# Rounded weight halves brought by a converting DMA on the Pool queue, with every fourth remainder subtracted on GpSimd

## The chip, the core and the metric

The kernel runs on one core of one Trainium2 chip. The metric is the time on the device, in microseconds, from the start of the program to its end. The matrix engine (TensorE, "PE" in the profile), the vector engine (VectorE, "DVE"), the scalar engine (ScalarE, "ACT"), GpSimd ("POOL") and the engine that issues most DMAs (SyncE, "SP") run side by side and wait for one another through semaphores. Sixteen DMA engines move the data between device memory and the on-chip memory.

## The reference

The program is a two-layer transformer trunk over 256 tokens of width 2048, all in float32. What matters here is that nearly all of the work is products of a small activation with large weights, each of which is used once.

```python
# x: (1, 256, 2048); layer 0: gated linear attention + MLP, layer 1: stick-breaking attention + MLP
h = x
h = h + gla_mixer(rms_norm(h, norm1_g[0]), gla_w_in[0], ..., gla_w_out[0])
h = h + jnp.square(jax.nn.relu(rms_norm(h, norm2_g[0]) @ mlp_w_up[0])) @ mlp_w_down[0]
k_sh, v_sh = shared_kv(h, kv_norm_g, kv_w)
h = h + stick_breaking_mixer(rms_norm(h, norm1_g[1]), sb_w_q[0], k_sh, v_sh, sb_w_out[0])
h = h + jnp.square(jax.nn.relu(rms_norm(h, norm2_g[1]) @ mlp_w_up[1])) @ mlp_w_down[1]
return rms_norm(h, final_g)        # mlp_w_up: (2, 2048, 8192), mlp_w_down: (2, 8192, 2048)
```

## The kernel before

Every weight is cut into units of 1 MB, 128 partitions by 2048 float32 values. The list `plan` holds the 361 units in the order of their use: 49 of the linear attention's input, 16 of its output, 128 of the first MLP, 8 and 16 of keys, values and queries, 16 of the second output projection, and 128 of the second MLP. SP loads a unit into a tile `raw`, of which there are three.

TensorE multiplies float32 data in a form with a short mantissa (float32r). To keep the precision, each weight is used as the sum of two such numbers. Each unit is taken as two halves of 128x1024. For a half, `prefetch` makes `wh`, the weight rounded to float32r (line 147, a cast on ScalarE), and `wl`, the remainder `raw - wh` (line 148, a subtraction on VectorE). There are three buffers of `wh` and three of `wl`. `next_half` calls `prefetch` until three halves are ready, and takes the first. So the buffers of half i+3 are those of half i, and they come free when TensorE has ended half i.

The activations are split in the same way, and stand as `[high | low]` beside each other. A unit whose weights are stationary (`unit_t`: names `up`, `qk`, `sq`, `sk`, lines 169 and 172) runs two matmuls for each of its 16 blocks of 128 rows: `wh` against 512 columns, `wl` against 256. A unit whose weights move (`half_n`: names `dn`, `op`, `v`, `r`, `sv`, lines 202 to 204) runs three matmuls of 512 columns for each pair of a block and a token tile: low tokens by `wh`, high tokens by `wh`, high tokens by `wl`. So in either kind both parts are needed almost as soon as a half begins: `wl` is read by the first, the second or the third matmul.

The MLP runs in four passes for each layer: 16 units `up` (each followed by `joined`, the sum of two halves of a PSUM bank: a copy `lo` on ScalarE, line 187, and the sum `s` on VectorE, line 188, then the squared ReLU `y` and its split into `hT`), and 16 units `dn` (each chunk of four followed by two additions to `h`, line 572). Other work (attention scores, norms) is handed out in steps by `pump` between the weight products. The last eight halves have buffers of their own (`stay`), because the last chunk runs one token tile after the other.

The order on each engine is that of a scheduler, which starts from the order of the code. Each engine works its own list in that order, and an instruction that waits holds up all that stand behind it on its engine.

Of the kernel before, what the change touches and what calls it, by code (L numbers as in the profile page):

```python
# [8 lines left out]
F32 = mybir.dt.float32  # L9
# [4 lines left out]
ALU = mybir.AluOpType  # L14
# [25 lines left out]
def yoco_kernel(ctx: ExitStack, tc: tile.TileContext, a: dict):  # L40
    nc = tc.nc
    V, S, PE = nc.vector, nc.scalar, nc.tensor

    # one table set serves every function used here
    S.preload_act_table_set("natural_log_exp_and_others")
# [6 lines left out]
    half = ctx.enter_context(tc.tile_pool(name="half", bufs=4))  # L52
# [5 lines left out]
    def t512(name, dt=F32):  # L58
        return tmp.tile([P, 512], dt, tag="t512", name=name)

    def t256(name):
        return half.tile([P, T], F32, tag="t256", name=name)
# [4 lines left out]
    def act_tile(name, pool=None):  # L67
        return (pool or actp).tile([P, KT, 2 * T], F32R, tag="act", name=name)

# [1 line left out]
    pending = []  # L71
    given = [0]
# [9 lines left out]

    # the first n given out so far have to be complete
    def drain(n=None):
        while pending and (n is None or given[0] - len(pending) < n):
            pump()
# [4 lines left out]

    # ---- weights: every unit is loaded whole, then split in halves, exactly, into a
    # 12-bit part and the rest; splits are issued ahead of the products that use them ----
    def out_order(w):
        return [w[c, i] for c in (0, 1) for i in range(3)] + [w[c, 3] for c in (0, 1)] + \
            [w[c, i] for c in (2, 3) for i in range(4)]
# [8 lines left out]
    plan = []  # L105
# [14 lines left out]
    before, between = {}, {}  # L120

    def prefetch():
        i = state["n"]
        if i == 2 * len(plan):
            return
        state["n"] += 1
        if i % 2 == 0:
            for todo in before.pop(i // 2, []):
                todo()
            raw = wraw.tile([P, 2048], F32, tag="raw", name="raw")  # L130
            for lo, hi in ((0, 512), (512, 1024), (1024, 2048)) if i == 0 else ((0, 2048),):
                nc.sync.dma_start(raw[:, lo:hi], plan[i // 2][:, lo:hi])
                for todo in between.pop((i, hi), []):
                    todo()
            state["raw"] = raw
        part = state["raw"][:, (i % 2) * 1024:(i % 2 + 1) * 1024]
        last = i - 2 * len(plan) + 8
        if last < 0:
            wh = wsp.tile([P, 1024], F32R, tag="wh", name="wh")
            wl = wsp.tile([P, 1024], F32R, tag="wl", name="wl")  # L140
        else:
            # the last chunk's products come one token tile after the other: all its weights stay
            if last == 0:
                state["stay"] = [act_tile(n).rearrange("p k t -> p (k t)") for n in ("stay_h", "stay_l")]
            wh, wl = [b[:, last * 1024:(last + 1) * 1024] for b in state["stay"]]
        for lo, hi in ((0, 512), (512, 1024)) if i == 0 else ((0, 1024),):
            S.copy(wh[:, lo:hi], part[:, lo:hi])  # L147
            V.tensor_tensor(wl[:, lo:hi], part[:, lo:hi], wh[:, lo:hi].bitcast(F32), op=ALU.subtract)  # L148
        ready.append((wh, wl))
# [8 lines left out]

    # out[feature, token]: weights stationary, [high | low] tokens moving
    def unit_t(act, name, steps=1):  # L160
# [22 lines left out]

    # sum of the two halves of a bank
    def joined(ps, out, rows=P):
        lo = t256("lo")
        S.copy(lo[0:rows], ps[0:rows, T:2 * T])  # L187
        V.tensor_tensor(out, ps[0:rows, 0:T], lo[0:rows], op=ALU.add)  # L188

    # out[token, column chunk]: tokens stationary, weights moving  # L190
    def banks(name):
        return [psA.tile([P, 512], F32, tag="psA", name=f"{name}{t}") for t in range(NT)]
# [23 lines left out]

    # a tile as the sum of two that the tensor engine takes in one pass
    def split(src, tile):
        hi, lo = tile("hi"), tile("lo")
        S.copy(hi, src)  # L220
        V.tensor_tensor(lo, src, hi.bitcast(F32), op=ALU.subtract)
        return hi, lo
# [8 lines left out]

    # 1 / sqrt(u), one Newton step behind the tables
    def rsqrt(u, out):
# [9 lines left out]

# [1 line left out]
    ident = const.tile([P, P], F32, name="ident")  # L245
    ones = const.tile([P, P], F32, name="ones")
# [19 lines left out]

# [1 line left out]
    xg = act_tile("xg")  # L268
# [48 lines left out]

    # a value per token, from partitions to the free axis of all partitions
    def spread(col, out, scale):
# [6 lines left out]

    # transposed, scaled and split: what the next products read
    def feed(c, targets):
# [29 lines left out]

# [1 line left out]
    oT = act_tile("oT")  # L360

    # scores of one head: decayed queries and keys, level by level; every exponent is at most 0
    def scores(hd, qT, kT, st, sx):
# [21 lines left out]

        # between the two token tiles, and on the diagonal
        e = t512("e0").rearrange("p (f t) -> p f t", f=2)
# [19 lines left out]

        # within them: keys of a pair's first half against queries of its second
        for lv, s in enumerate(LEVELS):
            if lv % 4 == 0:  # L410
                ps = psm("lev").rearrange("p (l t c) -> p l t c", l=4, t=NT)
            n = min(4, len(LEVELS) - lv // 4 * 4)
# [27 lines left out]

    # outputs of one head, its norm, the gate
    def outputs(hd, st, sx, vv, gs):
# [42 lines left out]

    # the output gate times the head's gain
    def gates(pss):
# [117 lines left out]

# [1 line left out]
    rstd, _ = squared_rstd(ssq, "rstd2")  # L607
# [26 lines left out]

    # one group of heads; keys on partitions, (head, query) along the free axis
    def sticks(n, qs):
        heads = slice(n * GRP, (n + 1) * GRP)

        # scores of a key tile against a query tile
        def score(qt, kt):  # L640
# [11 lines left out]

        # softplus, split: the products below have a side of ones and zeros
        def soft(z):
# [7 lines left out]

        # less everything between the key (itself too) and the query
        def weigh(z, own, later=None):
# [45 lines left out]
    for n in range(KVH):  # L710
        qs = [t512(f"q{t}") for t in range(NT)]
        for g in range(GRP):
            ps = unit_t(xq, "sq", 1 + (len(pending) > 1 or g == GRP - 1))
            s = t256("s")
# [50 lines left out]

# ---- layouts: stationary units [feature tile][partition][k tile, 128], moving units
# [1 line left out]
def _stationary(w):  # L768
# [17 lines left out]
def _lay_out(i):  # L786
# [27 lines left out]
    r["final_g"] = np.ascontiguousarray(i["final_g"])  # L814
    # constants of the shapes alone
    r["ident"] = np.eye(P, dtype=np.float32)
    at = np.arange(P)
# [4 lines left out]
    for s in LEVELS:  # L822
        second = at[at // s % 2 == 1][None, :]
# [20 lines left out]
```

## Time and profile before

| | |
|---|---|
| time, median of 2 runs | 2115.03 us (2114.76 to 2115.30) |
| span of the profiled execution | 2113.3 us |
| PE busy | 2097.4 us, 99% of the span |
| weight loads of PE (PEld) | 1763.1 us, 83% |
| DVE busy | 1313.0 us, 62% |
| ACT busy | 1039.5 us, 49% |
| POOL busy | 0.2 us |
| DMA moved | 388.40 MB, mean 184 GB/s |
| casts `wh`, line 147 | 715 + 8, 1051 ns each |
| subtractions `wl`, line 148 | 715 + 8, 1224 ns each |

Some instruction records overlap in time on PE, so its busy time is an upper reading. An engine's busy time says how much it does, and not whether anything waits for it; that is read from the waits and from the chain that ended last. The span leaves out about 1.7 us around the program that the time of a run contains.

### The profile page before, as it was taken

Reading aid. Unit: us, or ns where it says so; the run is one execution under the profiler, and the core shown is the slowest. Engines: PE = TensorE matmul, PEld = TensorE weight load, DVE = VectorE, ACT = ScalarE, POOL = GpSimd, SP = SyncE. Lnnn points to the kernel's source line nnn. Section 1 sums busy time; section 2 is a strip of 40 time slices with the busy share of each in tenths; the row PEclk is TensorE's granted clock in tenths of the full one; section 3 lists DMA queues with packets and bytes.
Section 4 is the critical chain, followed back from the end, with each engine's and each line's share of the span. In section 5 each row is a group of like instructions: output and inputs, shape, how many; then the busy total and the mean of one; then the engine's idle time right before and its main releaser. Section 6 shows DMA issues by size and latency. Waiting matters only on the chain.

```text
span 2113.3 us, 26650 instructions
## 1 busy us (share of the span) xinstructions
PE 2097.4 (99%) x10544; PEld 1763.1 (83%) x10544; DVE 1313.0 (62%) x1804; ACT 1039.5 (49%) x1447; POOL 0.2 (0%) x4
## 2 busy tenths in 40 slices
PE   8999999999999999999999999999999999999998
PEld 7888888888888888888888888888888888888886
DVE  5767876665566556556666687666556546655655
ACT  5645655544344344434455487544344434434443
POOL 0000000000000000000000000000000000000000
PEclk9999999999999999999999999999999999999999
DMA  8544444555555555555555644455555555555553
GB/s 313 180 160 160 156 164 157 182 180 188 192 194 183 188 191 181 197 189 190 182 182 178 216 142 156 165 188 188 193 187 190 187 186 192 181 197 185 193 182 137
DMA packets 55741, 388.40 MB, mean 184 GB/s; under 512 B 6448, under 2 KB 6960, under 8 KB 9152
## 3 DMA queue, kind: packets, MB, share of 16 engines
q1 hardware_dynamic: 55616, 386.70, 53.3%
q8 instruction: 83, 1.36, 0.3%
q14 instruction: 42, 0.34, 0.0%
HBM read 384.58 MB, written 2.10 MB: 183 GB/s over the span
## 4 chain that ended last, share of the span: by engine, by line
PE 98%; DVE 0%; ACT 0%; DMA 0%; SPq 0%; issue 0%; DVEq 0%
PE up L169 23%; PE up L172 11%; PE dn L204 11%; PE dn L203 11%; PE dn L202 11%; PE sq L169 3%; PE op L204 3%; PE op L202 3%; PE op L203 3%; PE qk L169 3%; PE sq L172 1%; PE r L202 1%; PE r L204 1%; PE r L203 1%; PE v L204 1%; PE v L202 1%
## 5 line engine op out<-in xcount | busy, mean ns | idle before, releaser
L148 DVE TENSOR_TENSOR wl<-raw,wh 128x1024 fp32r<-128x1024 f32 (+1 forms) x715 | 874.6, 1224 | 593.2 <-ACT wh L147 580.7
L147 ACT CAST wh<-raw 128x1024 fp32r<-128x1024 f32 (+1 forms) x715 | 751.2, 1051 | 725.9 <-PE dn L203 392.0
L169 PE MATMUL up<-xm,wh 128*128 128x512 f32 x2048 | 714.7, 398 | 0.0
L172 PE MATMUL up<-xm,wl 128*128 128x256 f32 x2048 | 554.5, 281 | 0.0
L169 PEld LDWEIGHTS up<-xm,wh 128*128 128x128 f32 x2048 | 376.8, 188 | 84.0
L172 PEld LDWEIGHTS up<-xm,wl 128*128 128x128 f32 x2048 | 386.8, 189 | 10.8
L204 PE MATMUL dn<-wl,hT 128*128 128x512 f32 x992 | 390.3, 393 | 0.0
L203 PE MATMUL dn<-wh,hT 128*128 128x512 f32 x992 | 389.0, 392 | 0.0
L202 PE MATMUL dn<-wh,hT 128*128 128x512 f32 x992 | 387.5, 391 | 0.0
L203 PEld LDWEIGHTS dn<-wh,hT 128*128 128x128 f32 x992 | 186.2, 188 | 42.6
L202 PEld LDWEIGHTS dn<-wh,hT 128*128 128x128 f32 x992 | 186.2, 188 | 41.3
L204 PEld LDWEIGHTS dn<-wl,hT 128*128 128x128 f32 x992 | 186.2, 188 | 40.8
L187 ACT COPY lo<-up 128x256 f32<-128x256 f32 x128 | 47.7, 373 | 227.6 <-PE up L169 227.6
L188 DVE TENSOR_TENSOR s<-up,lo 128x256 f32<-128x256 f32 x128 | 54.4, 425 | 118.4 <-ACT lo L187 118.4
L202 PE MATMUL op<-wh,oT 128*128 128x512 f32 x256 | 101.1, 395 | 0.0
L203 PE MATMUL op<-wh,oT 128*128 128x512 f32 x256 | 101.0, 395 | 0.0
L204 PE MATMUL op<-wl,oT 128*128 128x512 f32 x256 | 100.7, 394 | 0.0
L169 PE MATMUL sq<-xq,wh 128*128 128x512 f32 x256 | 91.0, 396 | 0.0
L169 PE MATMUL qk<-xg,wh 128*128 128x512 f32 x256 | 90.5, 397 | 0.0
L172 PE MATMUL qk<-xg,wl 128*128 128x256 f32 x256 | 69.9, 283 | 0.0
L172 PE MATMUL sq<-xq,wl 128*128 128x256 f32 x256 | 69.4, 280 | 0.0
L202 PE MATMUL v<-wh,xg 128*128 128x512 f32 x128 | 51.7, 404 | 6.3 <-ACT wh L147 6.3
(206 smaller groups left out, 1838.2 us busy)
## 6 DMA issues: line engine op xcount, KB each, us to landing
raw<-in_w_up SPq DMA_DIRECT2D x128, 1024.0 KB, 4.9
raw<-in_w_down SPq DMA_DIRECT2D x128, 1024.0 KB, 4.9
raw<-in_w_r SPq DMA_DIRECT2D x16, 1024.0 KB, 4.9
raw<-in_w_out SPq DMA_DIRECT2D x16, 1024.0 KB, 4.8
raw<-in_w_sq SPq DMA_DIRECT2D x16, 1024.0 KB, 4.8
raw<-in_w_so SPq DMA_DIRECT2D x16, 1024.0 KB, 5.0
raw<-in_w_v SPq DMA_DIRECT2D x15, 1024.0 KB, 4.9
raw<-in_w_q SPq DMA_DIRECT2D x8, 1024.0 KB, 4.9
```

The costliest lines, as they stand in the source:

```text
L147: S.copy(wh[:, lo:hi], part[:, lo:hi])
L148: V.tensor_tensor(wl[:, lo:hi], part[:, lo:hi], wh[:, lo:hi].bitcast(F32), op=ALU.subtract)
L169: PE.matmul(ps, wh[:, o:o + P], act[:, kt, :], start=first, stop=last)
L172: PE.matmul(ps[:, 0:T], wl[:, o:o + P], act[:, kt, 0:T], start=False, stop=False)
L187: S.copy(lo[0:rows], ps[0:rows, T:2 * T])
L188: V.tensor_tensor(out, ps[0:rows, 0:T], lo[0:rows], op=ALU.add)
L202: PE.matmul(pss[t], xl, wh[:, o:o + CH], start=kt == 0, stop=False)
L203: PE.matmul(pss[t], xh, wh[:, o:o + CH], start=False, stop=False)
L204: PE.matmul(pss[t], xh, wl[:, o:o + CH], start=False, stop=kt == KT - 1)
```

## The change

Of every half from the fifth on (`i >= 4`), `wh` is no longer cast on ScalarE from `raw`. Instead a DMA on the Pool queue reads the same 128x1024 values a second time from device memory and writes them into `wh` as float32r. `raw` is still loaded by SP as before, since the remainder needs it. Of every fourth half (`i % 4 == 3`) the remainder is subtracted on GpSimd instead of VectorE. Buffers, matmuls and their order stay.

```diff
@@ -39,9 +39,9 @@
-    V, S, PE = nc.vector, nc.scalar, nc.tensor
...
+    V, S, PE, G = nc.vector, nc.scalar, nc.tensor, nc.gpsimd
...
@@ -139,13 +139,17 @@
             wh, wl = [b[:, last * 1024:(last + 1) * 1024] for b in state["stay"]]
+        src = plan[i // 2][:, (i % 2) * 1024:(i % 2 + 1) * 1024]
         for lo, hi in ((0, 512), (512, 1024)) if i == 0 else ((0, 1024),):
-            S.copy(wh[:, lo:hi], part[:, lo:hi])
-            V.tensor_tensor(wl[:, lo:hi], part[:, lo:hi], wh[:, lo:hi].bitcast(F32), op=ALU.subtract)
+            if i < 4:
+                S.copy(wh[:, lo:hi], part[:, lo:hi])
+            else:
+                G.dma_start(wh[:, lo:hi], src[:, lo:hi])
+            (G if i % 4 == 3 else V).tensor_tensor(wl[:, lo:hi], part[:, lo:hi], wh[:, lo:hi].bitcast(F32), op=ALU.subtract)
         ready.append((wh, wl))
```

The remaining lines of the difference take comments away, so that the lines behind them stand four further down in the changed kernel (line 169 becomes 173, and so on).

How the lists of the engines change is shown at one place, where a pass of the first MLP begins with its `up` units. The numbers behind the names are those of the tiles: `raw_7783` is one unit, with the halves `wh_7785` and `wh_7805`; `raw_7834` is the next, with `wh_7836` and `wh_7856`; `raw_7885` has `wh_7887` and `wh_7907`. In the brackets stand the semaphores waited for: DMAHW those of SP's transfers, DMASW those of the Pool queue.

ScalarE before, from the first of these halves on:

```order
L147 CAST wh_7785<-raw_7783 128x1024 [waits DMAHW3_49,DVE_49,PE_49]
L147 CAST wh_7805<-raw_7783 128x1024 [waits DVE_49,PE_49]
L187 COPY lo_7826<-up_7782 128x256 [waits PE_49]
L147 CAST wh_7836<-raw_7834 128x1024 [waits DMAHW4_49,DVE_49]
L563 CAST hT_7781<-y_7829 128x256 [waits DVE_49]
L147 CAST wh_7856<-raw_7834 128x1024 [waits PE_49,Activation_49]
L187 COPY lo_7877<-up_7833 128x256 [waits PE_49]
L147 CAST wh_7887<-raw_7885 128x1024 [waits DMAHW5_49,Activation_49]
```

ScalarE now, at the same place:

```order
L191 COPY lo_7826<-up_7782 128x256 [waits PE_49,Activation_49]
L567 CAST hT_7781<-y_7829 128x256 [waits DVE_49]
L191 COPY lo_7877<-up_7833 128x256 [waits PE_49,Activation_49]
L567 CAST hT_7781<-y_7880 128x256 [waits DVE_49]
L191 COPY lo_7928<-up_7884 128x256 [waits PE_49,Activation_49]
```

The casts of the weights have gone from it, and the copies of `joined` and the casts of `hT` stand alone.

The Pool queue had no instruction there before; this is its list now:

```order
L151 DMA wh_7785<-in_w_up0 128x1024 [waits DMASW5_49,DVE_49,PE_49]
L152 TENSOR_TENSOR wl_7764<-raw_7745,wh_7763 128x1024 [waits DMAHW2_49,DMASW7_49]
L151 DMA wh_7805<-in_w_up0 128x1024 [waits DMASW6_49,DVE_49,PE_49]
L151 DMA wh_7836<-in_w_up0 128x1024 [waits PE_49,Pool_49]
L151 DMA wh_7856<-in_w_up0 128x1024 [waits DMASW0_49,DVE_49,PE_49]
L151 DMA wh_7887<-in_w_up0 128x1024 [waits DMASW1_49,DVE_49,PE_49]
L152 TENSOR_TENSOR wl_7857<-raw_7834,wh_7856 128x1024 [waits DMAHW4_49,DMASW3_49]
L151 DMA wh_7907<-in_w_up0 128x1024 [waits DMASW2_49,DVE_49,PE_49]
```

Each DMA waits for TensorE and for the subtraction that read its buffer three halves earlier. The subtraction of every fourth half (`wl_7857`) stands behind the DMA of the half after it (`wh_7887`) and ahead of the DMA of the next (`wh_7907`), and waits for the transfer of `wh_7856` (DMASW3).

VectorE before, at the same place:

```order
L148 TENSOR_TENSOR wl_7786<-raw_7783,wh_7785 128x1024 [waits DMAHW3_49,Activation_49]
L148 TENSOR_TENSOR wl_7806<-raw_7783,wh_7805 128x1024 [waits Activation_49]
L188 TENSOR_TENSOR s_7825<-up_7782,lo_7826 128x256 [waits Activation_49]
L562 SCALAR_TENSOR_TENSOR y_7829<-s_7825 128x256 [waits DVE_49]
L148 TENSOR_TENSOR wl_7837<-raw_7834,wh_7836 128x1024 [waits DMAHW4_49,Activation_49]
L564 TENSOR_TENSOR hT_7781<-y_7829,hT_7781 128x256 [waits Activation_49]
L148 TENSOR_TENSOR wl_7857<-raw_7834,wh_7856 128x1024 [waits Activation_49]
L188 TENSOR_TENSOR s_7876<-up_7833,lo_7877 128x256 [waits Activation_49]
```

VectorE now:

```order
L152 TENSOR_TENSOR wl_7786<-raw_7783,wh_7785 128x1024 [waits DMAHW3_49,DMASW0_49,DVE_49]
L192 TENSOR_TENSOR s_7825<-up_7782,lo_7826 128x256 [waits Activation_49]
L152 TENSOR_TENSOR wl_7806<-raw_7783,wh_7805 128x1024 [waits DMASW1_49,DVE_49]
L566 SCALAR_TENSOR_TENSOR y_7829<-s_7825 128x256 [waits DVE_49]
L568 TENSOR_TENSOR hT_7781<-y_7829,hT_7781 128x256 [waits Activation_49]
L152 TENSOR_TENSOR wl_7837<-raw_7834,wh_7836 128x1024 [waits DMAHW4_49,DMASW2_49,Pool_49]
L192 TENSOR_TENSOR s_7876<-up_7833,lo_7877 128x256 [waits Activation_49]
```

Its subtractions wait for the Pool queue's transfers where they waited for ScalarE, and `wl_7857` has moved to GpSimd.

## Rows read from the trace of the kernel before

**Rows 1.** The page: busy time and share of the span, instructions.

```profile
span 2113.3 us, 26650 instructions
...
PE 2097.4 (99%) x10544; PEld 1763.1 (83%) x10544; DVE 1313.0 (62%) x1804; ACT 1039.5 (49%) x1447; POOL 0.2 (0%) x4
```

**Rows 2.** Waits of PE over the span: engine, line, awaited, us in total, times, longest.

```profile
PE v L202 <- ACT wh L147: 6.3, 1, 6.3
PE v L204 <- DVE wl L148: 0.5, 1, 0.5
```

**Rows 3.** Timeline, a pass of `dn` (890 to 897 us): start, duration, engine, line.

```profile
891.36 1.06 ACT L147 CAST wh<-raw 128x1024 fp32r<-128x1024 f32 x1 [1.66 <-PE dn L203]
...
892.45 1.23 DVE L148 TENSOR_TENSOR wl<-raw,wh 128x1024 fp32r<-128x1024 f32 x1 [1.50 <-ACT wh L147]
...
894.08 1.06 ACT L147 CAST wh<-raw 128x1024 fp32r<-128x1024 f32 x1 [1.66 <-PE dn L203]
```

**Rows 4.** Timeline, a pass of `up` (599.6 to 606 us).

```profile
599.72 1.05 ACT L147 CAST wh<-raw 128x1024 fp32r<-128x1024 f32 x1 [1.98 <-PE up L169]
...
605.42 1.05 ACT L147 CAST wh<-raw 128x1024 fp32r<-128x1024 f32 x1 [1.14 <-PE up L169]
```

**Rows 5.** The page's DMA queue: packets, MB, share of 16 engines' span.

```profile
DMA packets 55741, 388.40 MB, mean 184 GB/s; under 512 B 6448, under 2 KB 6960, under 8 KB 9152
...
q1 hardware_dynamic: 55616, 386.70, 53.3%
```

**Rows 6.** DMA issues over the span: count, KB each, median us to landing.

```profile
raw<-in_w_up SPq DMA_DIRECT2D x128, 1024.0 KB, 4.9
...
out<-h SPq DMA_DIRECT2D x8, 256.0 KB, 2.5
```

**Rows 7.** DMA issues in the first 45 us: count, KB each, median us to landing.

```profile
raw<-in_w_r SPq DMA_DIRECT2D x4, 1024.0 KB, 7.2
raw<-in_w_v SPq DMA_DIRECT2D x3, 1024.0 KB, 8.1
...
raw<-in_w_v SPq DMA_DIRECT2D x1, 512.0 KB, 6.5
```

**Rows 8.** Windows: us, busy of PE, PEld, DVE, ACT, POOL, granted clock, DMA share, GB/s.

```profile
5.00:10.00 5.00, 3.68 (x9) 2.48 (x10) 3.42 (x8) 2.44 (x5) 0.00 (x0) 1.00 0.97 355
10.00:15.00 5.00, 4.48 (x20) 3.25 (x19) 3.07 (x3) 3.53 (x6) 0.00 (x0) 1.00 1.01 410
15.00:20.00 5.00, 5.00 (x24) 4.14 (x23) 4.79 (x9) 4.29 (x8) 0.00 (x0) 1.00 1.02 423
...
600.00:630.00 30.00, 30.00 (x173) 26.06 (x172) 19.10 (x26) 14.68 (x21) 0.00 (x0) 1.00 0.54 182
```

**Rows 9.** Groups by form: busy us, mean ns of one, idle before.

```profile
L148 DVE TENSOR_TENSOR wl<-raw,wh 128x1024 fp32r<-128x1024 f32 x713 | 873.2, 1225 | 592.0 <-ACT wh L147 579.5
...
L382 DVE TENSOR_TENSOR_SCAN cum<-scanm,mn 128x512 f32<-128x512 uint8 x4 | 4.9, 1224 | 0.1
```

**Rows 10.** SP's waits over the span.

```profile
SPq L132 <- DVE wl L148: 1821.5, 342, 10.1
```

## Prediction

> **What bounds the kernel now.** I read the page first. PE is busy for 2097.4 of 2113.3 us, and ACT, whose casts the change takes away, for half of the span [rows 1]. Then the waits: in the whole span PE waits for a cast once, for 6.3 us at the start, and for a subtraction for 0.5 us [rows 2]. So TensorE alone sets the time, and neither ACT nor DVE is ever late after the start. A change that relieves ACT can give back at most the 15.9 us in which PE is idle, 0.8%. The question is whether the new way of making the halves is still early enough.
>
> How early the old way is can be read off the timeline. In a pass of `dn` a cast begins every 2.72 us (891.36, 894.08), each released by the last matmul that reads the buffer (PE dn L203), and takes 1.06 us; the subtraction follows at once and takes 1.23 us [rows 3]. In `up`, two halves last 605.42 - 599.72 = 5.70 us, 2.85 each [rows 4]. I call the length of a half h. Half i+3 can begin to be made when half i ends, and TensorE wants it when half i+2 ends, 2h later: 5.44 us in `dn`, 5.70 in `up`. The old way takes 1.06 + 1.23, about 2.4 us with hand-offs, so some 3 us are to spare.
>
> **What is removed.** 719 casts leave ACT (723 less the first four halves), and 180 of the subtractions leave DVE. Both engines had the slack shown above, so this gives nothing. DVE keeps 3 in 4 subtractions.
>
> **What is added: a transfer in place of a cast.** The first 1.06 us of the chain become X, the time from the start of the Pool queue's DMA to the landing of 512 KB. No row shows a Pool DMA, so I bound it. SP's 1 MB load lands 4.9 us after its issue, and the 256 KB stores after 2.5 [rows 6]; on the line between them 512 KB takes 3.3 us. That is with the DMA engines half idle. The lower end is therefore 3.3. The upper end is a loaded machine: in the first 45 us a 512 KB piece of a unit took 6.5 us, and whole units 7.2 and 8.1 instead of 4.9 [rows 7].
>
> Which of the two is near? The weights are now read twice. SP's queue moved 386.70 MB in 53.3% of the span [rows 5], so its engines ran at 386.70 MB / 1126 us = 343 GB/s while busy; fully loaded they reached 410 to 423 (10 to 20 us) [rows 8]. The Pool queue adds 719 x 0.524 = 377 MB. In two halves of the MLP (5.57 us) the engines would have to move 2.10 MB, that is 376 GB/s: more than their rate with one load at a time and 89% of the highest rate seen. So most transfers meet another. If a 512 KB transfer shares the engines with a `raw` load for all of its data (0.524 MB / 343 GB/s = 1.5 us) it takes 3.3 + 1.5 = 4.8 us. To this comes what GpSimd needs to prepare the transfer, beyond what SP's landing times contain: between nothing and the 1.5 us that the data itself takes, and I take 0.8. **X = 5.6 us**, with 3.3 and 6.5 + 0.8 = 7.3 as ends.
>
> The Trainium skill, DMA: Bandwidth & Descriptors, section on the anatomy of one DMA on the gpsimd path, fits such a DMA by 2.0 us plus its bytes over 436 GB/s, which gives 3.2 us here, as an estimate. That speaks for the lower end; no run here shows it yet. By 3.2 the sum below would give about 2145 us, which is the second rival's case.
>
> **What is added: GpSimd's subtraction.** Call it s. DVE takes 1.23 us for the same operation, which is the lower end; the costliest operation per column in the trace is the scan, 1.224 us for 512 columns [rows 9], so 2.45 us for 1024, which I take as the upper end. GpSimd has done nothing in this trace but four tiny fills, and with nothing that excludes a slow engine I take **s = 2.4**, near the upper end.
>
> **What queues behind it.** The Pool list runs: transfer of half 4k+3, transfer of 4k+4, subtraction of 4k+3, transfer of 4k+5. The subtraction waits for the landing of its own transfer, and the next transfer stands behind it. Ordinary halves need X + 1.23 + 0.2 (hand-offs) = 7.0 us against 2h = 5.6, and halves with GpSimd's part 5.6 + 2.4 + 0.2 = 8.2. Both are late. What a group of four then costs: the transfer of half 4k+3 starts when half 4k ends (its buffer); X + s + 0.2 later half 4k+3 is ready; TensorE runs it and half 4k+4, and at the end of 4k+4 the same begins again with the transfer of half 4k+7. So the loop over four halves lasts X + s + 0.2 + 2h instead of 4h, and the loss for each four is X + s + 0.2 - 2h. The ordinary halves fit inside: the transfer of 4k+5 starts when the subtraction ends (8.2 us after half 4k), and its half is ready 7.0 us later, at 15.2; half 4k+4 ended at 13.8. That is 1.4 us late, but the next loop's own half 4k+7 comes only at 13.8 + 8.2 = 22.0, and halves 4k+5 and 4k+6 still fit ahead of it (15.2 + 2 x 2.8 = 20.8). So I add nothing for them.
>
> SP is touched too: a `raw` buffer comes free only when both of its subtractions are done, and SP already waits for these 342 times, 1821.5 us in all [rows 10]. Later subtractions mean later loads, but there are three `raw` buffers, six halves, and a load needs 4.9 us, so this costs nothing until a load is over 6 us late.
>
> **The sum.** The MLPs hold 256 of 361 units, 512 halves, 128 groups of four, with h = 2.79 (mean of 2.72 and 2.85): each loses 5.6 + 2.4 + 0.2 - 5.57 = 2.63 us, 337 us in all. The other 210 halves take 2113 - 512 x 2.785 = 687 us, 3.27 each, since attention work lies between them; there the loss is 8.2 - 6.54 = 1.66 us for each of 52 groups, 86 us. Together 423 us on a median of 2115 (the profiled span, 2113.3, and 1.7 around it): **2540 us**, 20% slower. With X = 4.4 and s = 1.8 it is 128 x 0.83 = 106 us, 2220; with both upper ends 9.95 us for each group, 128 x 4.38 + 52 x 3.41 = 738 us, 2855.
>
> **Rivals.**
>
> *Hidden, so no change.* If X is 3.3 and s at most 2.0, then X + s + 0.2 = 5.5 us, under 2h, and TensorE never waits: 2115 to 2155 us. For it: the landing times of lone transfers. Against it: 376 GB/s are wanted where one load at a time gives 343, so transfers can't stay alone. It decides at X + s = 5.4 us.
>
> *Bandwidth alone.* The buffers are no bound, but the engines keep to 343 GB/s: (388 + 377) / 343 = 2230 us. Against it: the start of the trace shows 410 and 423.
>
> *Converting is slow.* The DMA engines may rewrite each value at half of the copying rate. No row shows a converting DMA. Then 377 MB need 2200 us at 171 GB/s and the loads 1126 more, 3325 us; scaled to 423 GB/s the two are 1783 + 914 = 2700.
>
> *GpSimd and DVE get in each other's way.* If GpSimd's subtraction can't run beside one of DVE's, s grows by up to 1.23 us, 180 x 1.23 = 221 us more: 2760. The rows can't speak to it, since POOL was idle. The Trainium skill, SBUF — State Buffer, section Who interferes with whom, says that a VectorE instruction with two inputs in SBUF and a GpSimd instruction that reads SBUF exclude each other for the whole instruction. `wl` on DVE has two such inputs; no run here shows it so far.
>
> **How the numbers follow.** Forecast (loop through the Pool queue, 2220 to 2855) 0.53; exclusion on top of it, 0.10; slow conversion (2700 to 3325) 0.18; bandwidth alone 0.10; hidden 0.08; some gain that I don't see, 0.01. All but the last two are over 2% slower, and 2% is about what a measurement of this kernel can tell from no change: slower 0.91, same 0.08, faster 0.01. The range 2190 to 3150 leaves out the hidden case below and not quite half of the slow conversion above, 0.17 together.
>
> **What the profile would show.** Right: PE's waits name the weights' parts, with DMA `wh` and POOL `wl` ahead, PE's busy share near 83%, its wait longest before each fourth half, Pool transfers landing after 5 to 6 us, SP's loads after over 5, ACT near 290 us busy. The granted clock, 1.00 in these stretches [rows 8], stays there, since the waits are 1 to 3 us; if they brought the clock down to its lower level of 1.2 GHz, the time would be far above the range. Hidden: landing near 3.3 us and no waits of PE. Slow conversion: a DMA share at 95% or more with total GB/s below 300. Wrong in a part: if all halves wait alike, the ring of three buffers and not GpSimd's place in the queue is the bound.

## The result and the profile after

The changed kernel takes 2899.45 us (median of two runs, 2897.39 to 2901.51) against 2115.03: 1.371 times as long, interval [1.3669, 1.3748]. It is 785 us slower. The forecast was 2540, 425 us slower, with a range up to 3150. So sign and range held, and the forecast loss was little more than half of what came.

The page of the changed kernel, its lines on busy time, on the DMA queues and on the chain that ended last:

```profile
span 2899.7 us, 26994 instructions
...
PE 2374.4 (82%) x10544; PEld 1855.1 (64%) x10544; DVE 1259.8 (43%) x1624; ACT 318.1 (11%) x729; POOL 815.6 (28%) x902
...
q0 software_dynamic: 103392, 376.48, 40.0%
q1 hardware_dynamic: 55616, 386.70, 38.4%
...
DMA 33%; issue 23%; POOL 12%; PE 9%; DVE 6%; ACT 0%; POOLq 0%; DVEq 0%; ACTq 0%
```

PE, 99% busy before [rows 1], is busy for 82%, and part of that is work at the lower clock: the mean granted clock fell from 0.999 to 0.934. ACT has only 318 us left, and nothing came of it. The loads and the transfers keep the DMA engines busy for 78% of the span (53.3% before [rows 5]). A third of the chain that ended last is DMA; before, 98% of it was PE's own work and 0% DMA.

PE's waits in the changed kernel (engine, line, awaited, us in total, times, longest), which answer to [rows 2]:

```profile
PE up L176 <- DVE wl L152: 133.3, 59, 5.5
PE dn L206 <- DMA wh<-in_w_down: 96.8, 65, 3.3
PE up L176 <- POOL wl L152: 76.7, 61, 5.7
PE dn L208 <- DVE wl L152: 43.7, 70, 2.6
PE dn L208 <- POOL wl L152: 25.0, 16, 1.7
```

The weights' parts are awaited, as forecast. But the lines for GpSimd's subtraction (POOL `wl`), which the forecast made the heart of the loss, hold 102 us; those for DVE's subtractions, which stand behind the ordinary transfers, and for the transfers themselves hold 274.

The issues and landings (count, KB each, median us from issue to landing), and GpSimd's subtraction by form (busy us, mean ns of one, idle before):

```profile
raw<-in_w_up SPq DMA_DIRECT2D x128, 1024.0 KB, 5.9
wh<-in_w_up POOLq DMA_DIRECT2D x256, 512.0 KB, 5.3
raw<-in_w_down SPq DMA_DIRECT2D x128, 1024.0 KB, 6.1
wh<-in_w_down POOLq DMA_DIRECT2D x248, 512.0 KB, 5.2
```

```profile
L152 POOL TENSOR_TENSOR wl<-raw,wh 128x1024 fp32r<-128x1024 f32 x178 | 431.3, 2423 | 169.2 <-DMA wh<-in_w_down 53.7 <-DMA wh<-in_w_up 48.2 <-DMA wh<-in_w_so 13.8
```

X = 5.6 us and s = 2.4 us, the two unknown prices, are met by the median landing of 5.2 to 5.3 and by 2.42.

**Where the loss lies.** From the first to the last cast of `hT` in a pass of `up` (15 units) it was 84.7 us and is 118.7, the mean of eight passes: 2.26 us for each unit, 4.5 for a group of four halves. From the last of these casts to the first of the next pass (16 units `dn` and one `up`) it was 93.5 and is 131.9: again 2.26 for a unit. So the MLPs lose 128 x 4.5 = 580 us (forecast 337), the rest 205, 3.9 for a group (forecast 86, 1.66 for a group).

Now a stretch of `dn`, 757 to 785 us of the changed kernel, its timeline (start, duration, engine, line; in brackets the idle time before and what ended it):

```profile
758.40 0.53 POOL L151 DMA_DIRECT2D wh<-in_w_down  x1 [4.32 <-PE dn L208]
758.95 2.40 POOL L152 TENSOR_TENSOR wl<-raw,wh 128x1024 fp32r<-128x1024 f32 x1
761.29 0.57 POOL L151 DMA_DIRECT2D wh<-in_w_down  x1
761.37 0.33 SPq L132 DMA_DIRECT2D raw<-in_w_down  x1
761.40 0.19 PEld L208 LDWEIGHTS dn<-wl,hT 128*128 128x128 f32 x1 [0.32 <-POOL wl L152]
...
767.62 0.53 POOL L151 DMA_DIRECT2D wh<-in_w_down  x1 [2.77 <-PE dn L207]
770.21 0.19 PEld L206 LDWEIGHTS dn<-wh,hT 128*128 128x128 f32 x1 [3.09 <-DMA wh<-in_w_down]
...
771.57 0.50 PE L208 MATMUL dn<-wl,hT 128*128 128x512 f32 x1 [0.63 <-DVE wl L152]
775.75 0.53 POOL L151 DMA_DIRECT2D wh<-in_w_down  x1 [7.60 <-PE dn L208]
776.29 2.40 POOL L152 TENSOR_TENSOR wl<-raw,wh 128x1024 fp32r<-128x1024 f32 x1
```

In the forecast's numbering GpSimd's half is 4k+3. 758.40 is the transfer of 4k+4, which waited for PE to end a half; behind it stands the subtraction of 4k+3, and behind this, at 761.29, the transfer of 4k+5. GpSimd's half itself is 0.3 us late (761.40). The long wait is for 4k+5: its transfer is awaited until 770.21, for 8.9 us. The end of GpSimd's subtraction lets two things go at once, this transfer and SP's load (761.37), since the subtraction was the last reader of a `raw` buffer. They run together, for part of the time beside the transfers of 4k+4 and 4k+6 too. Then DVE can begin its own subtraction, for which PE waits until 771.57; then the half runs, and its end, at 775.75, releases the next transfer that stands ahead of a subtraction. So the loop that PE waits for is

- issue and GpSimd's subtraction, 758.40 to 761.29: 2.89 us,
- landing of the transfer that starts with SP's load, to 770.21: 8.92,
- DVE's subtraction and half 4k+5, to 775.75: 5.54; together 17.35.

I took the same three parts of all 121 groups of the MLPs that show them in the trace:

| part, us | shortest group (of `dn`) | median `up`, `dn` | mean `up`, `dn` |
|---|---|---|---|
| issue and subtraction | 2.88 | 3.06, 2.89 | 3.79, 3.86 |
| landing of 4k+5's transfer | 6.3 | 6.4, 6.5 | 6.96, 7.07 |
| DVE's subtraction and the half | 4.01 | 4.70, 4.08 | 5.23, 4.60 |
| group of four | 13.2 | 16.14, 15.45 | 15.98, 15.53 |

The means are the loss: four halves took 11.4 us in `up` and 10.9 in `dn` [rows 3, 4], so 4.6 us more. The landing of this one transfer goes up to 9.9. From 560 to 1040 us it is issued within 0.1 us of an SP load 30 times, and lands after 7.0 us in the median; the 93 others land after 4.8.

Windows of the changed kernel (us, busy of PE, PEld, DVE, ACT, POOL, granted clock, DMA share, GB/s):

```profile
564.00:566.00 2.00, 0.09 (x1) 0.00 (x0) 0.00 (x0) 0.00 (x0) 0.53 (x1) 1.00 0.92 299
568.00:570.00 2.00, 2.00 (x8) 1.71 (x8) 1.56 (x2) 0.37 (x1) 0.00 (x0) 0.50 0.73 174
```

Here PE waited for 3.6 us, until 567.6, and then ran at 0.50 of its clock, 1.2 GHz instead of 2.4, with matmuls of 0.63 us instead of 0.40. This is a second thing that the forecast ruled out. Over the span it can have cost (1 - 0.934) x 2900 = 191 us at most. In the loop it shows in the third part: in `dn`, where the landing took under 7 us, DVE's subtraction and the half took 4.0 to 4.1 in 25 of 32 groups; where it took 8.5 us or more, 5.4 to 5.9 in 9 of 10. Mean less median of that part, 0.5 us of the 4.6 for a group, is about what the clock adds there.

### The profile page after: what moved, and what is told of

Its sections match the earlier page's. It is cut to its first block, busy times and chain, and to the rows that moved or that the text cites. A ratio compares the mean times of both kernels' runs of the same rounds, so it can differ in the third digit from the quotient of the medians.

```text
span 2899.7 us, 26994 instructions
## 1 busy us (share of the span) xinstructions
PE 2374.4 (82%) x10544; PEld 1855.1 (64%) x10544; DVE 1259.8 (43%) x1624; ACT 318.1 (11%) x729; POOL 815.6 (28%) x902
## 3 DMA queue, kind: packets, MB, share of 16 engines
q0 software_dynamic: 103392, 376.48, 40.0%
## 4 chain that ended last, share of the span: by engine, by line
DMA 33%; issue 23%; POOL 12%; PE 9%; DVE 6%; ACT 0%; POOLq 0%; DVEq 0%; ACTq 0%
DMA wh<-in_w_down 14%; DMA wh<-in_w_up 13%; POOL wl L152 11%; DVE wl L152 6%; POOL wh L151 2%; DMA wh<-in_w_so 2%; PE up L173 2%; PE dn L208 2%; DMA wh<-in_w_sq 1%; PE dn L206 1%; PE dn L207 1%; DMA wh<-in_w_out 1%; PE up L176 1%; PE sq L173 1%; DMA wh<-in_w_sk 1%
## 5 line engine op out<-in xcount | busy, mean ns | idle before, releaser
L152 DVE TENSOR_TENSOR wl<-raw,wh 128x1024 fp32r<-128x1024 f32 (+1 forms) x537 | 685.8, 1279 | 1219.6 <-DMA wh<-in_w_down 564.7
L173 PE MATMUL up<-xm,wh 128*128 128x512 f32 x2048 | 771.1, 420 | 0.0
L176 PE MATMUL up<-xm,wl 128*128 128x256 f32 x2048 | 596.1, 301 | 210.4 <-DVE wl L152 133.3
L206 PE MATMUL dn<-wh,hT 128*128 128x512 f32 x992 | 421.3, 425 | 97.4 <-DMA wh<-in_w_down 96.8
L208 PE MATMUL dn<-wl,hT 128*128 128x512 f32 x992 | 429.2, 433 | 70.1 <-DVE wl L152 43.7
L152 POOL TENSOR_TENSOR wl<-raw,wh 128x1024 fp32r<-128x1024 f32 x178 | 431.3, 2423 | 169.2 <-DMA wh<-in_w_down 53.7
L207 PE MATMUL dn<-wh,hT 128*128 128x512 f32 x992 | 411.4, 415 | 0.0
L151 POOL DMA_DIRECT2D wh<-in_w_up x256 | 137.6, 537 | 693.9 <-PE up L173 560.4
L151 POOL DMA_DIRECT2D wh<-in_w_down x248 | 133.4, 538 | 622.1 <-PE dn L208 336.9
L566 DVE SCALAR_TENSOR_TENSOR y<-s 128x256 f32<-128x256 f32 x128 | 129.5, 1012 | 2.3
L206 PE MATMUL op<-wh,oT 128*128 128x512 f32 x256 | 106.7, 417 | 20.9 <-DMA wh<-in_w_so 11.4
L567 ACT CAST hT<-y 128x256 fp32r<-128x256 f32 x128 | 52.0, 406 | 428.3 <-DVE y L566 428.3
```

What stands on the lines that cost most here:

```text
L151: G.dma_start(wh[:, lo:hi], src[:, lo:hi])
L152: (G if i % 4 == 3 else V).tensor_tensor(wl[:, lo:hi], part[:, lo:hi], wh[:, lo:hi].bitcast(F32), op=ALU.subtract)
L173: PE.matmul(ps, wh[:, o:o + P], act[:, kt, :], start=first, stop=last)
L176: PE.matmul(ps[:, 0:T], wl[:, o:o + P], act[:, kt, 0:T], start=False, stop=False)
L206: PE.matmul(pss[t], xl, wh[:, o:o + CH], start=kt == 0, stop=False)
L207: PE.matmul(pss[t], xh, wh[:, o:o + CH], start=False, stop=False)
```

## The experiments

Three theories stood after the result. **Loop:** the forecast's own, through the transfer and the subtraction of GpSimd's half. **Ring:** with three buffers a half has 2h = 5.44 to 5.7 us from a free buffer to its use, and a transfer with its subtraction needs about that or more, whoever subtracts. **Data:** the engines move twice as much, or convert slowly, and the buffers matter little. Each kernel below starts from the changed one unless it says otherwise, and ratios are against the kernel before.

**1. All remainders on DVE**

```diff
-            (G if i % 4 == 3 else V).tensor_tensor(wl[:, lo:hi], ...)
+            V.tensor_tensor(wl[:, lo:hi], ...)
```

> All remainders are subtracted on VectorE again; the converting transfers stay. If GpSimd's subtraction and what queues behind it is most of the loss (the forecast): only the ring of three buffers is left, where half i+3 is ready 5.2 + 1.23 + 0.2 = 6.6 us after half i, so three halves take 6.6 + 2.8 = 9.4 us, 3.13 each instead of 2.79; over 512 halves of the MLPs that is 2115 + 177, about 2290 us, with a granted clock back at 0.98 or more. If the second reading of the weights is the bound (bandwidth): the 765 MB are the same, and it stays over 2700 us.

2853.99 us, 1.350 [1.3441, 1.3559]. Taking GpSimd's subtraction out gives back some 45 us of 785, so it cannot be the cause of the whole. The time lies where the expectation put bandwidth (over 2700) and far above what it gave the bare ring (2290). Run 7 speaks against bandwidth: there the same data go through in 2426 us. Its timeline in a pass of `dn`:

```profile
718.35 13.86 SPq L132 DMA_DIRECT2D raw<-in_w_down  x3
...
722.43 0.53 POOL L151 DMA_DIRECT2D wh<-in_w_down  x1 [6.85 <-PE dn L207]
...
729.00 0.50 PE L206 MATMUL dn<-wh,hT 128*128 128x512 f32 x1 [1.01 <-DMA wh<-in_w_down]
729.50 2.36 DVE L152 TENSOR_TENSOR wl<-raw,wh 128x1024 fp32r<-128x1024 f32 x2 [8.32 <-DMA wh<-in_w_down]
730.78 0.50 PE L208 MATMUL dn<-wl,hT 128*128 128x512 f32 x1 [1.04 <-DVE wl L152]
733.42 0.53 POOL L151 DMA_DIRECT2D wh<-in_w_down  x1 [4.83 <-PE dn L208]
```

Here the ring is bare, with nothing of GpSimd's in it. A buffer comes free at 722.43, its transfer lets PE begin at 729.00, 6.6 us later, the remainder is ready at 730.78, the half ends at 733.42, and the buffer's next transfer begins. Three halves in 11.0 us, 3.67 each, 14.7 for four, where PE needs 10.9: nearly as long as the changed kernel's 15.5. The expectation had 9.4 for three; 1.3 of the 1.6 us between lie in this transfer, which lands after 6.5 us instead of 5.2. A load of SP was issued 1.2 us before it (the loads that the first line holds together are at 718.35, 721.21 and 731.88).

**2. GpSimd's subtraction alone, all casts on ScalarE**

```diff
-            if i < 4:
+            if True:
```

> All casts on ScalarE as before the change, no converting transfers; only every fourth remainder is subtracted on GpSimd. Forecast: cast 1.06 + subtraction 2.42 + 0.2 = 3.7 us is under 2h = 5.6, so no wait of TensorE, 2115 us within 1%. If GpSimd and VectorE exclude each other, it shows all the same in VectorE's durations: y and wl, 426 and 1225 ns each before, become longer when they meet one of GpSimd's, or GpSimd's own goes from 2.4 to over 3 us. If GpSimd's part alone is the cost, the time rises to 2300 us or more.

2125.21 us, 1.0047 [1.0032, 1.0062]. Where the old 3 us of slack stand, a subtraction of 2.48 us on GpSimd is hidden. The same run shows that GpSimd and DVE do exclude each other. Groups by form (busy us, mean ns):

```profile
L152 POOL TENSOR_TENSOR wl<-raw,wh 128x1024 fp32r<-128x1024 f32 x178 | 441.2, 2479 | 1640.3 <-ACT wh L149 1573.5 <-DVE e L424 20.7 <-PE op L208 12.6
L426 DVE TENSOR_TENSOR e<-e,kT 128x256 f32<-128x256 f32 x28 | 16.9, 604 | 1.2 <-ACT e L425 1.2
```

Before, `e` took 419 ns. The whole costs 10 us.

**3. Half 4k+3, GpSimd's, cast on ScalarE again; the other transfers and GpSimd's subtraction kept**

```diff
-            if i < 4:
+            if i < 4 or i % 4 == 3:
```

> The halves whose remainder GpSimd subtracts get wh by ScalarE's cast; the other three in four by converting transfer. If the loop goes through the own transfer of GpSimd's half (the forecast's loop, X + s + 0.2 - 2h for each four): that loop is gone, and with a quarter less to move about 2200 us. If the loop goes through the transfer that stands behind the subtraction on the Pool queue: 0.54 + 2.42 + 5.5 + 2.8 + 0.7 = 12.0 us for each four instead of 11.1, and TensorE's waits name the half behind GpSimd's: 2300 us or more.

2715.23 us, 1.283 [1.2799, 1.2862]. GpSimd's subtraction no longer waits for a transfer, so the forecast's loop has lost its X, and 600 of 785 us remain. Its timeline in a pass of `dn`:

```profile
939.91 1.05 ACT L149 CAST wh<-raw 128x1024 fp32r<-128x1024 f32 x1 [12.75 <-PE dn L207]
941.05 2.40 POOL L152 TENSOR_TENSOR wl<-raw,wh 128x1024 fp32r<-128x1024 f32 x1 [5.57 <-ACT wh L149]
943.39 0.57 POOL L151 DMA_DIRECT2D wh<-in_w_down  x1
949.94 0.50 PE L206 MATMUL dn<-wh,hT 128*128 128x512 f32 x1 [1.48 <-DMA wh<-in_w_down]
951.26 0.50 PE L208 MATMUL dn<-wl,hT 128*128 128x512 f32 x1 [0.58 <-DVE wl L152]
```

As the bound of the kernel the forecast's loop is refuted, and the one read from the changed kernel's timeline is here again, by a half earlier: the transfer that stands behind the subtraction is now that of 4k+4. It starts with an SP load (943.47), PE has it after 6.55 us, waits for DVE's subtraction to 951.26, and the end of that half releases the next cast for GpSimd. The next subtraction of GpSimd begins at 954.84, 13.8 us after the one before.

**4. Is a Pool transfer slow in itself? Plain loads in two halves of 1024 columns, from the Pool queue and from SP.** Both start from the kernel before.

```diff
-                nc.sync.dma_start(raw[:, lo:hi], plan[i // 2][:, lo:hi])
+                (nc.sync if i < 6 else nc.gpsimd).dma_start(raw[:, lo:hi], ...)
...
+        elif i >= 6:
+            nc.gpsimd.dma_start(state["raw"][:, 1024:2048], plan[i // 2][:, 1024:2048])
```

The second kernel has `nc.sync` for `nc.gpsimd` in both lines.

> The kernel before the change, with each unit loaded as two plain halves of 512 KB from the Pool queue instead of one 1 MB load from SP; ScalarE casts. Without a second stream beside it, a plain 512 KB transfer of the Pool queue lands after 4.1 us if the queue, and not the converting, makes the converting one slow, and after 3.3 us or less if the converting does. The time stays at 2115 us, since raw comes early enough.

> As the run with plain halves from the Pool queue, but from SP: 512 KB land after 3.3 us, as worked out from the 1 MB and 256 KB rows, and the time stays at 2115 us.

2116.41 us, 1.0005 [0.9996, 1.0015], and 2115.54 us, 1.0001 [0.9992, 1.001]. The landings of 512 KB, first from the Pool queue:

```profile
raw<-in_w_up POOLq DMA_DIRECT2D x256, 512.0 KB, 4.6
```

and from SP:

```profile
raw<-in_w_up SPq DMA_DIRECT2D x256, 512.0 KB, 4.5
```

In both kernels the two halves of most units are issued 0.4 to 0.5 us apart, so that these medians mix two cases: the first of such a pair lands after 4.2 us from the Pool queue and 3.9 from SP, the second after 5.0 and 4.9. So the queue makes a difference of 0.1 to 0.3 us, where the forecast put 0.8 for "what GpSimd needs to prepare the transfer"; and the 3.3 us that I drew from loads and stores [rows 6] was too low for either queue.

**5. Transfers without the second stream.** All remainders on DVE; SP loads only the first three units, and their three tiles stand for `raw` of all later ones, so that the second stream and its numbers are left out.

```diff
+            if i < 6:
+                raw = wraw.tile([P, 2048], F32, tag="raw", name="raw")
+                kept.append(raw)
+            raw = kept[i // 2 % 3]
...
+                if i < 6:
+                    nc.sync.dma_start(raw[:, lo:hi], plan[i // 2][:, lo:hi])
```

> All remainders on VectorE, three buffers, converting transfers as changed, but SP loads only the first three units and the remainders of all later halves are taken from these, so the second stream is left out. If a transfer is late because it meets SP's loads: it lands 3.3 to 4 us after its issue, 3.7 + 1.23 + 0.2 = 5.1 us is under 2h = 5.6, and the time is 2115 to 2170 us. If a converting transfer of the Pool queue takes over 5 us by itself: 2400 us or more.

2223.65 us, 1.0515 [1.0499, 1.0531].

```profile
q0 software_dynamic: 103392, 376.48, 61.1%
...
wh<-in_w_up POOLq DMA_DIRECT2D x256, 512.0 KB, 4.1
```

A converting transfer that meets nothing but its own kind lands after 4.1 us. With 1.23 for the subtraction and 0.2 for hand-offs that is 5.5 of the 5.44 to 5.7 us that the ring has: it just fits, and a loss of 109 us is left, between the two times expected. That this is what a ring without slack costs is argued and not shown. Against run 1, which differs only in SP's loads, 630 us have gone. So the second stream is what makes it expensive, by its amount or by how it meets the first. That the conversion halves the rate is excluded: 376.48 MB in 61.1% of 2223 us are 277 GB/s while busy, against 331 for the plain halves of the Pool queue in run 4, and in the changed kernel 376.48 MB in 40.0% of 2900 are 325, beside SP's 347.

**6. Amount or meeting? Fewer transfers, the rest cast, all remainders on DVE.** Three kernels, each with one of the three lines: transfers for the second halves of all units; for one half in four, a second half; for one half in four, a first half.

```diff
-            if i < 4:
+            if i < 4 or i % 2 == 0:
+            if i < 4 or i % 4 != 1:
+            if i < 4 or i % 4 != 0:
```

> Transfers for every second half only, ScalarE's cast for the others, all remainders on VectorE. The engines have 575 MB to move, at 337 GB/s 1706 us, 80% of the old time. If engine load and meeting streams are the cause: a transfer has one raw load beside it, lands in 5 us or less, 6.4 against 2h = 5.6 for one half in two, which the ring evens out in part: 2200 to 2350 us. If each transfer costs a fixed delay in the ring, half of the loss of the run with all transfers remains: 2480 us.

> Transfers for one half in four, ScalarE's cast for the others, all remainders on VectorE. 483 MB, 1430 us at 337 GB/s. If load is the cause: the landing is near 4 us, 5.4 against 5.6, 2115 to 2170 us. If each transfer costs a fixed delay: a quarter of the loss, 2300 us.

> Transfers for one half in four as in the run before, but the first half of a unit (i % 4 == 0) instead of the second (i % 4 == 1); the same bytes. The first half's transfer starts when half i-3, the second of a unit, ends, and that is when SP starts the next raw load. If a transfer is late because it starts together with a raw load: landing near 5 us instead of 4.0, and 2240 to 2330 us against 2184. If only the amount of data counts: 2184 us within 1%.

| transfers | time, us | ratio | landing of `wh`, us (`up`, `dn`) |
|---|---|---|---|
| every second half | 2492.35 | 1.177 [1.1731, 1.1809] | 5.2, 4.7 |
| every fourth, a second half | 2184.46 | 1.0326 [1.0305, 1.0346] | 4.0, 4.2 |
| every fourth, a first half | 2419.08 | 1.1425 [1.1395, 1.1455] | 5.6, 5.7 |

The first lies at the time expected if each transfer costs a fixed delay (2480). The last two don't: by a fixed delay both would have been 2300. They move the same 483 MB, and one loses 69 us, the other 304. The amount of data is not it. The timeline of the one with second halves, in `up`:

```profile
699.63 11.82 SPq L132 DMA_DIRECT2D raw<-in_w_down  x3
...
705.80 0.53 POOL L151 DMA_DIRECT2D wh<-in_w_up  x1 [11.15 <-DVE hT L568]
...
709.84 1.23 DVE L152 TENSOR_TENSOR wl<-raw,wh 128x1024 fp32r<-128x1024 f32 x1 [0.64 <-DMA wh<-in_w_up]
```

and of the one with first halves:

```profile
699.67 10.27 SPq L132 DMA_DIRECT2D raw<-in_w_up  x2
700.43 0.53 POOL L151 DMA_DIRECT2D wh<-in_w_up  x1 [12.21 <-PE up L173]
...
707.23 2.36 DVE L152 TENSOR_TENSOR wl<-raw,wh 128x1024 fp32r<-128x1024 f32 x2 [4.82 <-DMA wh<-in_w_up]
707.34 0.47 PE L173 MATMUL up<-xm,wh 128*128 128x512 f32 x1 [1.57 <-DMA wh<-in_w_up]
708.51 0.80 PE L176 MATMUL up<-xm,wl 128*128 128x256 f32 x2 [0.70 <-DVE wl L152]
```

In the first the transfer starts 3.2 us behind an SP load (the three that this row holds together are at 699.63, 702.59 and 711.13), in the second 0.8 us behind (699.67). So it is all along: from 560 to 1040 us, 42 of 42 transfers of the first kernel start 2.9 to 3.7 us behind a load and land after 4.05 us in the median, and 36 of 36 of the second 0.6 to 0.9 us behind and land after 5.7, at least 5.45. In the kernel with all second halves, from 560 to 1040 us, the 30 transfers that start within 1.3 us behind a load land after 5.8, and the 33 that start 6 us or more behind one after 4.1. What makes a transfer late is a load that starts with it. In the second kernel DVE then does two subtractions back to back: the next half's, though cast in time, stands behind the late one. Both kernels with one half in four missed the times that I gave them, the first by 14 us above its upper end, the second by 89: I had not counted the second half that is held up.

**7. A deeper ring: four buffers of `wh`, each transfer a half earlier,** the subtraction still when three are ready (`tmp` gives up two of 11 buffers for the space). `finish_half` subtracts. With GpSimd's subtraction; with all on DVE; with all on DVE and second halves alone by transfer:

```diff
-            wh = wsp.tile([P, 1024], F32R, tag="wh", name="wh")
+            wh = wsp.tile([P, 1024], F32R, tag="wh", name="wh", bufs=4)
...
+        staged.append((i, part, wh, wl))
...
-        while len(ready) < 3:
+        while len(ready) + len(staged) < 4:
...
+        while len(ready) < 3 and staged:
+            finish_half()
```

> As changed, but with four buffers of wh (three of wl), transfers issued one half earlier, and nine instead of eleven temporary tiles to make room. If latency in the ring and the queue is the cause: a half has 3h = 8.4 us for 5.3 + 1.23 + 0.2 = 6.7 us (8.0 with GpSimd's part), so most waits go: 2150 to 2300 us. If bandwidth is the bound: no change, over 2700 us.

> Four buffers of wh and all remainders on VectorE. With four buffers the 16 DMA engines were 88% busy at 2587 us, so at the same rate they need 2270 us without a pause. If the engines' total work is the bound there, taking GpSimd's subtraction out gives little: 2540 to 2590 us. If GpSimd's subtraction is what holds the queue up, the time falls to 2300 to 2400 us.

> Transfers for every second half (the odd ones, as in the run with every second half), all remainders on VectorE, and four buffers of wh. If the short ring is what makes late transfers cost (5.2 us landing + 1.3 against 2h = 5.6 with three buffers, 3h = 8.4 with four): 2115 to 2170 us against 2492 with three. If the load on the DMA engines costs by itself (575 MB): over 2300 us.

| four buffers | time, us | ratio | with three buffers |
|---|---|---|---|
| GpSimd's subtraction kept | 2587.39 | 1.2247 [1.2222, 1.2271] | 2899.45 |
| all on DVE | 2425.93 | 1.1485 [1.1444, 1.1527] | 2853.99 |
| all on DVE, second halves alone | 2273.19 | 1.0739 [1.072, 1.0757] | 2492.35 |

One buffer more gives back 312, 428 and 219 us, more than any other edit that keeps the transfers. So with three buffers the short ring is a large part of the loss, though the edit also lets each subtraction stand behind the next transfer, and no run takes the two apart. All three kernels missed their times: the first and the third lie between what I gave a short ring (2150 to 2300, 2115 to 2170) and the DMA engines (over 2700, over 2300), the second between the queue (2300 to 2400) and the engines' total work (2540 to 2590). Now GpSimd's subtraction costs 161 us where it cost 45: with three buffers the bare ring is nearly as long as the loop through GpSimd, and hides it. What is then late: the page of the second of these kernels, and SP's and Pool's landings:

```profile
q0 software_dynamic: 103392, 376.48, 47.9%
q1 hardware_dynamic: 55616, 386.70, 42.8%
...
raw<-in_w_up SPq DMA_DIRECT2D x128, 1024.0 KB, 7.6
wh<-in_w_up POOLq DMA_DIRECT2D x256, 512.0 KB, 6.5
```

The engines are busy for 91% and both streams land later than ever: here bandwidth looks like the next bound, but no run tests it. In the third kernel the engines have room (75%), and the loss that stays, 158 us, was foreseen by none of the theories; its cause is open. Its waits over the span show ACT waiting for the loads of `raw`, 7 us in all before the change:

```profile
ACT wh L150 <- DMA raw<-in_w_down: 216.1, 48, 7.7
```

## Why the prediction was right and wrong

**Nothing is given back by relieving ACT and DVE:** right; ACT fell from 49% to 11%, and the time rose.

**Sign and range:** that the range held is luck. The forecast's loop went from 2220 to 2855 us, and 2899 lies outside it; the room up to 3150 came from slow conversion, which run 5 excludes. PE's busy share "near 83%" is an accident too: it came out at 82%, but of 2374 us of busy time and not of 2097, since part of it ran at the lower clock.

**X and s:** right as medians (5.2 to 5.3 for 5.6; 2.42 for 2.4), but X by luck, since two of its parts were off in opposite ways: 3.3 for a lone transfer should have been 4.1, and of the 0.8 for GpSimd's preparation run 4 shows 0.1 to 0.3. The 1.5 us for a transfer that meets a load was near: 5.7 against 4.05 in run 6. The Trainium skill, DMA: Bandwidth & Descriptors, in its section on the anatomy of one DMA on the gpsimd path, gave an estimate of 3.2 us; the lone transfer of run 5 took 4.1, so the measurement decides against it here.

**The step that failed** is "The ordinary halves fit inside: ... So I add nothing for them". I had the transfer of 4k+5 behind GpSimd's subtraction, and its half late by 1.4 us, and let it hide in the loop through 4k+3 and its two halves. That rested on one X for all transfers. With X = 5.6 the loop through 4k+5 is 2.9 + 5.6 + 4.1 = 12.6 us, under the forecast's 13.8, and the step holds. But this transfer starts at the instant that SP's load starts, and lands after 7.0 on average: 14.0, while the forecast's own loop shrinks to 5.2 + 2.4 + 0.2 + 5.4 = 13.2. So 4k+5 is the bound, and what makes its landing longer adds to each group; GpSimd's subtraction waiting for its own landing in some groups adds 1.0, and the clock 0.5. That gives the 15.5 of `dn`. The prediction's test, "if all halves wait alike, the ring of three buffers and not GpSimd's place in the queue is the bound", came out between: in the changed kernel the place in the queue does set the loop, by another half than I said, and without GpSimd (run 1) the ring is nearly as bad. Outside the MLPs it is the same loop: 43 groups show the three parts with means of 4.5, 6.6 and 5.3 us, 16.4 in all, where the forecast had 13.1 before the change and 14.7 behind it.

**"The granted clock ... stays there"** was wrong: 0.934. At most 191 of the 360 us that are missing in the sum lie here, by the loop's third part about 0.5 us for a group, some 70 us in the MLPs; no run takes the clock apart from the late landings. That the time would be "far above the range" in that case was wrong too.

**SP's loads cost nothing:** in the sense meant there it was right; only the first and the last halves wait for `raw` in the changed kernel, some 17 us on all engines. What I missed is that these loads do harm by when they start and not by when they end: without them 630 us are gone (run 5), and with the same data the moment of the start is worth 235 (run 6).

**The rivals.** Hidden: no; its condition, X + s under 5.4, is not met, though with a single stream, and DVE alone to subtract, the loss is only 5% (run 5). Slow conversion: excluded by run 5. Bandwidth: not the bound of the changed kernel (78% busy, run 6's equal amounts, and run 7, which moves the same data in 2587 and 2426 us); that it is the next one is likely and not shown. Exclusion of GpSimd and DVE: real. In the changed kernel, the timeline of `up`:

```profile
572.87 2.39 POOL L152 TENSOR_TENSOR wl<-raw,wh 128x1024 fp32r<-128x1024 f32 x1
572.98 2.57 DVE L566 SCALAR_TENSOR_TENSOR y<-s 128x256 f32<-128x256 f32 x1
```

`y` takes 0.43 us in run 2; here it ends 0.3 us after GpSimd's instruction, and so do all 35 of them that begin under one. The Trainium skill, SBUF — State Buffer, section Who interferes with whom, says that a VectorE instruction with two inputs in SBUF and a GpSimd instruction that reads SBUF exclude each other, and the trace agrees. But here it is DVE that grows (`y` from 0.43 to 1.01 us in the mean) and not s, which stays at 2.42. The price was put too high: 221 us, where GpSimd's whole part is worth 10 with casts (run 2), 45 in the changed kernel (run 1) and 161 with four buffers (run 7).

Two slips change nothing: 718 casts leave ACT and not 719, as the first half's cast stands in two pieces; and 2145 us is the case of the first rival, "hidden", not of the second.

## What to carry to other kernels

When a 1 us instruction that fills a ring of buffers is replaced by a DMA, compare the ring's time (buffers less one, times the length of a step) with the DMA's latency and all that follows it, before any look at busy shares: 5.5 against 5.6 was lost as soon as a second stream ran. Look for the event that starts two streams at once, and price that transfer by itself, not by the median of all. Write down every loop through the queues: the bound was one that the forecast had listed and dismissed, and two loops of nearly the same length hide each other when one is taken away.

## What the runs showed of the hardware

- A plain load of 512 KB with another 0.4 to 0.5 us behind it lands after 3.9 us from SP and 4.2 from the Pool queue, one of 1 MB from SP after 4.9: from SP, half of the size takes 1 us off.
- The converting transfer is no slower to land (4.1 us in run 5), though the DMA engines move it at 277 GB/s while busy, against 331 for plain halves; GpSimd is busy for 0.53 us with each issue.
- A subtraction of 128x1024 float32 takes 2.42 us on GpSimd, 1.98 times DVE's 1.225 [rows 9].
- After a wait of PE of 3.6 us the granted clock was 0.50 for the matmuls that followed, so that a long wait costs more than its length.
- Two kernels with the same 483 MB differ by 235 us; in one the transfers start 2.9 to 3.7 us behind a load and land after 4.05 us, in the other 0.6 to 0.9 us behind and land after 5.7 (run 6).
